# One decoder block: silu pairs in the middle, a second gate product asked for earlier, y in freed h tiles, v pieces on GpSimd's queue

## The chip, the core and the metric

The kernel runs on one core of one Trainium2 chip. A core has a matrix engine (TensorE, here PE, with its weight load PEld), a vector engine (DVE), a scalar engine (ACT), GpSimd (POOL) and SyncE (SP), which here only issues transfers. All of them work on tiles of 128 partitions in on-chip memory; 16 DMA engines move data between it and device memory. The engines run in parallel, each takes its instructions in order, and semaphores hold an instruction until what it needs is there. The metric is the device time of one execution, in microseconds.

## What is computed

A residual block over 1024 positions and 1024 channels, in float32:

```python
h = rmsnorm(x) * (1 + scale) + shift              # scale, shift, gate from c
q, k, v, g_attn, xr, g_rnn, m_attn, m_rnn = split(h @ w_in)
y_attn = window_attention(rope(q), rope(k), v, sinks) * silu(g_attn)
xr = causal_conv4(xr)
r, i = sigmoid(xr @ wa + ba), sigmoid(xr @ wx + bx)   # 4 blocks of 256 channels
a = exp(-8 * r * softplus(-lam))
state[t] = a[t] * state[t-1] + sqrt(1 - a[t]**2) * i[t] * xr[t]
y_rnn = state * silu(g_rnn)
merged = sigmoid(m_attn) * (y_attn @ w_ap) + sigmoid(m_rnn) * (y_rnn @ w_rp)
out = rmsnorm(x + gate * (merged @ w_out))
```

The attention has 16 heads of 64 in four groups (one k and v head for each), a window of 128 positions and a learned sink per head.

## The kernel before

Every float32 factor is split into a high part, rounded to the matrix engine's float32r format, and a low rest; a product is three matmuls (high x high, low x high, high x low). The split is one ACT cast (`cast`, line 101) and one DVE subtraction (`rest`, line 107).

**Pairs.** The wide projection is done in pairs of 128-column chunks (`Pair`, line 509). A pair is computed as a 2 x 2 block product with seven products instead of eight, so it takes seven slots of 12 matmuls (`product`, line 500, matmuls at line 505), at a planner's cost of 2.75 us a slot. In the seven slots it needs sums of weights (`tsum`, line 527), seven splits, and copies and differences of results (lines 554, 557, 565). Its weights are loaded six slots ahead (`r`, a ring of six tiles). Four sinks of a pair take a finished result of 128 x 512 each:

- a q pair applies the rotary embedding and stores q;
- a tanh pair (`MA`, `MR`, the merge gates; `tanh_sinks` with `silu` false) is one ACT tanh (line 608), whose result is stored (a sigmoid is made of it at the end);
- a silu pair (`GA`, `GR`) is a tanh on ACT and then one DVE instruction (line 613), whose result is stored;
- an `XR` pair collects two channel blocks for the recurrent branch, whose convolution is four steps (`base` on ACT, line 682, and three `tap`s on DVE, line 687).

There are 23 pairs. The list `pairs` (line 249) sets their order; the pair with index i starts at slot 7i. The last pair, MR[3], runs inside the attention stage.

**Recurrent branch.** For each of the four `XR` pairs there are two gate products (`extra`, line 764, matmuls at line 778), 24 matmuls into two PSUM tiles each; PSUM has two tiles for them, so that a second product overwrites what the sigmoids of the first have read. `after_gates` (line 785) is the chain behind a product: sigmoids (793, 796) and d1 (799), tanh (807) and d2 (803), exp and square (810, 813), d3 (816), square root (820), d4 (823), the scan (828), a product with the stored silu(g_rnn) (832), and the split of y, which is stored as `yh_d` and `yl_d` (835, 839). Chain 0 and chain 1 of a pair come one after the other. `start_gates` asks for product 1 after the step of chain 0 with index 3.

**Order.** A planner at build time writes the order of all engines. Fixed steps stand at a slot (`at_slot`); background steps wait in two lists (`waiting`) and are placed at a slot where the planned load of ACT and DVE (`Load`) leaves room (`background`, line 468). `slots(1)` in a list means that the next step comes at least one slot later; the last chains (hb = 3, "rush") have none between their steps. Where the lists are empty and slot 150 or so is reached, `open_attn` (line 968) starts attention.

**Attention stage.** There are 32 units of one group and 128 positions. In unit u the scores of u are made (line 1016), weights of u - 1 (1040), the values of u - 3 (1088) and the transposes of u - 2 (1054); POOL sets the sink column (`sink`, 1004) and the masks (1074). Between these PE takes one piece of other work a unit: the slots of the last pair, and then `rp_steps` (line 1150), the product of y with w_rp, in 32 pieces. SP loads ks and qs for every second unit, the two v factors (`load_v`, line 991, called from `values` at every second unit), the stored silu(g_attn), w_rp, and y: `load_y(0)` and `load_y(1)` go into tiles of h that are already free, chunks 2 to 7 into a ring `ypool` of 12 tiles. `store` (line 590) puts off the stores of this stage to the next `flush`, on SP. After attention come the w_ap products, the merge and the output product; the merged chunks are written to y's tiles (chunks 0 and 1) or to the ring.

Of the kernel before, what the change touches and what calls it, by code (L numbers as in the profile page):

```python
# [13 lines left out]
F32R = mybir.dt.float32r  # L14
# [8 lines left out]
P = 128  # L23
S = 1024
# [23 lines left out]
SL = [slice(0, HALF), slice(HALF, S)]  # L48
# [3 lines left out]
def tile_hybrid_block(ctx, tc, x, pk, rows, posr, posi, invf, c_row, w_ss, w_gate, w_main, w_v,  # L52
                      w_g, w_ap, w_rp, w_out, out):
    nc = tc.nc
# [83 lines left out]

    hba = ctx.enter_context(tc.tile_pool(name="hba", bufs=1))
    h_ctx = ExitStack()  # L140
    hb = h_ctx.enter_context(tc.tile_pool(name="hb", bufs=1))
    b12_ctx = ExitStack()
    b12 = b12_ctx.enter_context(tc.tile_pool(name="b12", bufs=1, side="right"))
    hh, hl = [], []
    for kc in range(KC):
        for lst, nm in ((hh, "hh"), (hl, "hl")):
            if kc < 4:
                a = hba.tile([P, HALF], F32R, name=f"{nm}a{kc}")
                b = b12.tile([P, HALF], F32R, name=f"{nm}b{kc}")
                lst.append([a[:], b[:]])  # L150
            else:
                a = hb.tile([P, S], F32R, name=f"{nm}{kc}")
                lst.append([a[:, SL[0]], a[:, SL[1]]])
    xx = b12_ctx.enter_context(tc.tile_pool(name="xx", bufs=1, side="right"))
    hx = h_ctx.enter_context(tc.tile_pool(name="hx", bufs=8))
    xT = [xx.tile([P, S], F32, name=f"xT{kc}") if kc % 4 == 3 else
# [444 lines left out]
    def tanh_sinks(dst, silu):  # L601
        def steps(j, th):
            def sink(s):
                t = {}

                def f1():
                    t["t"] = blk()
                    A.activation(t["t"], s(), AF.Tanh, scale=0.5)
                    if not silu:
                        store(dst[j][:, SL[th]], t["t"])  # L610

                def f2():
                    V.scalar_tensor_tensor(out=t["t"], in0=t["t"], scalar=1.0, in1=s(),
                                           op0=ALU.add, op1=ALU.mult)
                    store(dst[j][:, SL[th]], t["t"])

                return [("A", 0.62, 0, f1)] + ([("D", 0, 0.69, f2)] if silu else [])
            return sink
        return {"C11": steps(0, 0), "C12": (blk, steps(0, 1)), "C21": steps(1, 0),
                "C22": (blk, steps(1, 1))}  # L620
# [38 lines left out]
    def xr_sinks(hb):  # L659
# [15 lines left out]
        def conv(ic):  # L675
            def add(s):
                c, t = 2 * hb + ic, {}
                x_ = xr[ic]

                def base():  # L680
                    t["xc"] = W["rn"].tile([P, S], F32, tag="xc", name="xc", bufs=2)
                    A.activation(t["xc"][:], x_[:], AF.Identity,
                                 scale=pcol(PK_CW + 24, c), bias=pcol(PK_CB, c))

                def tap(k):
                    o = t["xc"][:, 3 - k:]
                    V.scalar_tensor_tensor(out=o, in0=x_[:, :S - 3 + k],
                                           scalar=pcol(PK_CW + 8 * k, c), in1=o,
                                           op0=ALU.mult, op1=ALU.add)

                def hi():
                    t["h"] = W["rn"].tile([P, S], F32R, tag="xa", name="xch", bufs=2)
                    A.copy(t["h"][:], t["xc"][:])

                def lo():
                    t["l"] = W["rn"].tile([P, S], F32R, tag="xcl", name="xcl", bufs=2)
                    V.tensor_tensor(out=t["l"][:], in0=t["xc"][:], in1=f32(t["h"][:]),
                                    op=ALU.subtract)
                    W["xc", hb, ic] = (t["h"], t["l"], t["xc"])

                taps = [("D", 0, 1.28, lambda k=k: tap(k)) for k in (2, 1, 0)]
                waiting[1].extend([[("A", 1.06, 0, base)], slots(1), *[[t_] for t_ in taps]])
                load0, split0 = gate_weights(hb, 0)
                if ic == 1:
                    waiting[1].append(load0)
                waiting[1].extend([slots(1), [("A", 1.06, 0, hi)], slots(1),
                                   [("D", 0, 1.22, lo)]])
                if ic == 1:
                    waiting[1].extend(split0 + [lambda: start_gates(hb)])
            return add  # L710
# [30 lines left out]
    def ask(hb, oc):  # L741
# [2 lines left out]
            gq.append((hb, oc))  # L744
        return ("g", (hb, oc)) in W

    def start_gates(hb):

        load1, split1 = gate_weights(hb, 1)
# [2 lines left out]
        one, two = [], [lambda: ask(hb, 1)]  # L752
        for todo, steps_ in ((one, c0), (two, c1)):
            for i, step in enumerate(steps_):
                todo.extend(step + ([slots(1)] if hb < 3 else []))
                if todo is one and i == 3:
                    todo.append(lambda: gq.append((hb, 1)) or True)
        if hb == 3:
            one.insert(0, lambda: W.setdefault("rush", True))
        waiting[0].extend(one + two)  # L760
# [2 lines left out]

    def extra():

        if not gq or Load.pe < W.get(("ready", *gq[0]), 1e9):
            return 0.0
        hb, oc = gq.pop(0)
        wh, wl = W["gw", hb, oc]
# [15 lines left out]
    def after_gates(hb, oc):  # L785
# [16 lines left out]
        def d2():  # L802
            V.tensor_tensor(out=t["it"][:], in0=t["it"][:], in1=W["xc", hb, oc][2][:],
                            op=ALU.mult)

        def a3():
            A.activation(tl("th"), t["rz"][:], AF.Tanh)
# [183 lines left out]
    def load_v(m):  # L991
        g, n0 = m // 4, (m % 4) * 2
        vs = at.tile([P, 2, P], F32R, tag="vs", name="vs", bufs=2)
        dv = at.tile([P, 2, P], F32R, tag="dv", name="dv", bufs=2)
        dma(dv[:], dv_d[g][:, n0:n0 + 2, :])
        lo = 0 if n0 else 1
        dma(vs[:, lo:, :], vs_d[g][:, n0 - 1 + lo:n0 + 1, :])
        U["v", m] = vs, dv

    def sink(u):  # L1000
# [134 lines left out]
    def load_y(c):  # L1135
        if c < 2:
# [3 lines left out]
                dma(ls[i], yl_d[c][:, SL[i]])  # L1140
            yh[c], yl[c] = hs, ls
            return
        h_ = W["yp"].tile([P, S], F32R, tag="Y", name="yh")
        l_ = W["yp"].tile([P, S], F32R, tag="Y", name="yl")
        dma(h_[:], yh_d[c])
        dma(l_[:], yl_d[c])
        yh[c] = [h_[:, SL[0]], h_[:, SL[1]]]
        yl[c] = [l_[:, SL[0]], l_[:, SL[1]]]

    def rp_steps():  # L1150
# [1 line left out]
        pb_ctx.close()  # L1152
        psr = pool(ctx, "psr", space=PSUM, side="right")
        rp_acc.extend(psr.tile([P, S], F32, name=f"rp{i}") for i in range(2))
        W["yp"] = pool(ctx, "ypool", bufs=12)
        W["tout"] = pool(ctx, "tout", bufs=1)
        W["hpool"] = pool(ctx, "hpool", bufs=7)

# [14 lines left out]

        seq = [(c, k) for k in range(4) for c in range(2)]
        seq += [(c, k) for c in range(2, KC) for k in range(4)]
        load_y(2)
        load_y(3)
        for i, (c, k) in enumerate(seq):
            part(c, k)
# [35 lines left out]
    def a_prep(m):  # L1215
# [13 lines left out]
        def f3():  # L1229
# [4 lines left out]
            else:  # L1234
# [11 lines left out]
    GR = [Pair(C_GR + 2 * g, tanh_sinks(sgr_d[2 * g:2 * g + 2], True)) for g in range(NG)]  # L1246
    XR = [Pair(C_XR + 2 * h, xr_sinks(h)) for h in range(4)]
    Q = [None] + [Pair(2 + 2 * g, rope_q(g), 0.125) for g in range(1, NG)]
    pairs = [Q[1], MA[0], Q[2], MA[1], Q[3],
             XR[0], GR[0], GR[1], XR[1], MA[2], GR[2], MR[0], XR[2], MR[1], MR[2], MA[3],  # L1250
             XR[3], GR[3]] + GA + MR[3:]
    N_ATT = 1
    def v_product(ps, th):
        for kc, i in [(kc, i) for j in range(2) for kc in range(KC) for i in (j, j + 2)]:
# [67 lines left out]
    while W["slot"] < 7 * (len(pairs) - N_ATT) + 1:  # L1322
# [1 line left out]
        flush()  # L1324

    s_last = 7 * len(pairs) - 7
    at_slot(s_last + 2, ("N", 0, 0, lambda: load_r(0)), ("N", 0, 0, lambda: load_y(0)),
            ("N", 0, 0, lambda: load_r(1)), ("N", 0, 0, lambda: load_y(1)),
            ("N", 0, 0, lambda: prep_r(0, 0)), ("N", 0, 0, lambda: prep_r(1, 0)))

    def fill():
        for _ in steps:
# [116 lines left out]
    for c in range(KC):  # L1449
# [17 lines left out]
        V.scalar_tensor_tensor(out=s_[:], in0=s_[:], scalar=1.0, in1=ps[:], op0=ALU.add,  # L1467
                               op1=ALU.mult)
        V.tensor_tensor(out=t[:], in0=t[:], in1=s_[:], op=ALU.add)
        if c < 2:  # L1470
            mh[c], ml[c] = yh[c], yl[c]
        else:
            mh[c], ml[c] = [
# [161 lines left out]
```

## Time and profile before

| | us |
|---|---|
| median of 3 runs | 946.4 (944.32 to 946.92) |
| profiled execution | 944.47 |
| its span, first to last instruction | 942.5 |
| PE busy | 908.1 (96%) |
| DVE busy | 688.8 (73%) |
| ACT busy | 528.8 (56%) |
| POOL busy | 89.7 (10%) |

The span lies 1.97 us under the time of the same execution. The profile names an instruction by engine, source line, operation and "out<-in". In the views of stages there is the busy time of each engine in a stretch of the span; in the views of waits, how long an engine stood still and which instruction released it; in the timeline, start, duration and in brackets the idle time ahead with its releaser. A transfer issued at SP has the engine name SPq. The stages lie as follows: start to about 101 us, pairs and recurrent branch to 570, attention from 570 to 760 (the last pair to 603, the w_rp products from 605), then the w_ap products and the merge to 845, and the output product.

### The profile page before, as it was taken

The numbers are of one execution on the slowest core, as the hardware profiler recorded it, in microseconds if no ns is written. First come the engines' busy times: TensorE is split into PE (matmuls) and PEld (weight loads), VectorE is DVE, ScalarE is ACT, GpSimd is POOL, SyncE is SP. The second block draws the span as 40 slices with busy tenths as digits, with TensorE's granted clock in tenths as the row PEclk, the third lists the DMA queues.
The fourth block names the chain that finished last, engine by engine and source line by source line (L and its number), as shares of the span: only waits on it lengthen the run. The fifth ranks groups of instructions, "written<-read, shape, count | busy, mean of one in ns | idle before, by whom it ended". The sixth has DMA issues, their size and how long they took to land.

```text
span 942.5 us, 12419 instructions
## 1 busy us (share of the span) xinstructions
PE 908.1 (96%) x4261; PEld 750.6 (80%) x4261; DVE 688.8 (73%) x1068; ACT 528.8 (56%) x1036; POOL 89.7 (10%) x129
## 2 busy tenths in 40 slices
PE   5899999999999999999999999989999999999997
PEld 3689777788888788888888778867888888887886
DVE  7977798876668955984688677888999737656522
ACT  7434654455556755866585775877888632212311
POOL 1056000000000000000000000233333300000000
PEclk9999999999999999999999999999999999999999
DMA  8923565753332433352334237897666286436321
GB/s 312 370 68 152 184 223 202 268 189 125 112 112 96 139 136 100 133 212 80 122 112 168 100 134 261 278 342 251 215 198 187 67 304 219 168 118 235 128 79 67
DMA packets 84275, 164.19 MB, mean 174 GB/s; under 512 B 12771, under 2 KB 33251, under 8 KB 84214
## 3 DMA queue, kind: packets, MB, share of 16 engines
q1 hardware_dynamic: 83350, 161.09, 49.8%
q0 software_dynamic: 720, 2.07, 0.6%
q8 instruction: 33, 0.54, 0.2%
q14 instruction: 28, 0.23, 0.1%
q10 hardware_dynamic: 144, 0.26, 0.1%
HBM read 114.00 MB, written 49.78 MB: 174 GB/s over the span
## 4 chain that ended last, share of the span: by engine, by line
PE 75%; ACT 4%; DMA 4%; DVE 4%; issue 2%; SPq 0%; POOL 0%; DVEq 0%; ACTq 0%
PE bk L505 39%; PE rp L168 12%; PE rp L1500 5%; PE pgate L778 5%; PE pmain L1500 4%; PE pmain L168 4%; PE s_ps L1016 3%; PE pv L1088 3%; PE pt L1054 1%; DMA dv<-dv_d 1%; DMA ks<-k_d 1%; DMA r<-w_rp 1%; ACT wh L101 1%; DMA r<-w_main 1%; DVE nl L390 1%
## 5 line engine op out<-in xcount | busy, mean ns | idle before, releaser
L505 PE MATMUL bk<-nh,wl 128*128 128x512 f32 x368 | 143.7, 391 | 2.0 <-DVE wl L107 1.9
L505 PE MATMUL bk<-nh,wh 128*128 128x512 f32 x368 | 143.4, 390 | 0.0
L505 PE MATMUL bk<-nl,wh 128*128 128x512 f32 x368 | 143.2, 389 | 0.0
L107 DVE TENSOR_TENSOR wl<-r,wh 128x512 fp32r<-128x512 f32 x108 | 79.1, 736 | 16.5 <-ACT wh L101 16.5
L101 ACT CAST wh<-r 128x512 fp32r<-128x512 f32 x108 | 66.5, 618 | 33.5 <-DMA r<-w_ap 11.3
L505 PEld LDWEIGHTS bk<-nh,wl 128*128 128x128 f32 x368 | 69.1, 188 | 17.7 <-DVE wl L107 3.1
L505 PEld LDWEIGHTS bk<-nh,wh 128*128 128x128 f32 x368 | 69.1, 188 | 15.2 <-ACT wh L103 0.9
L505 PEld LDWEIGHTS bk<-nl,wh 128*128 128x128 f32 x368 | 69.1, 188 | 14.3
L505 PE MATMUL bk<-hh,wl 128*128 128x512 f32 x184 | 71.7, 390 | 0.4 <-DVE wl L107 0.4
L505 PE MATMUL bk<-hl,wh 128*128 128x512 f32 x184 | 71.6, 389 | 0.0
L505 PE MATMUL bk<-hh,wh 128*128 128x512 f32 x184 | 71.6, 389 | 0.0
L107 DVE TENSOR_TENSOR wl<-ws,wh 128x512 fp32r<-128x512 f32 x80 | 54.1, 683 | 4.0 <-ACT wh L101 4.0
L101 ACT CAST wh<-ws 128x512 fp32r<-128x512 f32 x80 | 48.2, 616 | 4.8 <-DVE ws L527 3.0
L1040 ACT ACTIVATE p<-p,small 128x129 f32<-128x129 f32 x128 | 50.1, 400 | 0.0
L59 POOL DMA_DIRECT2D yh_d<-yh x1 | 0.6, 583 | 482.3 <-ACT yh L835 482.3
L505 PE MATMUL bk<-hha,wl 128*128 128x512 f32 x92 | 36.4, 395 | 5.9 <-DVE wl L107 4.4
L505 PEld LDWEIGHTS bk<-hh,wl 128*128 128x128 f32 x184 | 34.5, 188 | 7.9 <-DVE wl L107 0.8
L505 PEld LDWEIGHTS bk<-hh,wh 128*128 128x128 f32 x184 | 34.5, 188 | 7.2
L505 PEld LDWEIGHTS bk<-hl,wh 128*128 128x128 f32 x184 | 34.5, 188 | 7.1
L1016 PE MATMUL s_ps<-ks,qs 128*128 128x256 f32 (+1 forms) x256 | 37.5, 289 | 0.0
L1517 ACT ACTIVATE o<-xo 128x1024 f32<-128x1024 f32 (+2 forms) x10 | 8.9, 889 | 48.4 <-DVE xo L1516 48.4
L505 PE MATMUL bk<-hla,wh 128*128 128x512 f32 x92 | 35.9, 390 | 0.0
(338 smaller groups left out, 2231.7 us busy)
## 6 DMA issues: line engine op xcount, KB each, us to landing
r<-w_main SPq DMA_DIRECT2D x100, 256.0 KB, 4.0
wada<-w_ss SPq DMA_DIRECT2D x16, 512.0 KB, 8.6
qs<-q_d SPq DMA_DIRECT2D x16, 512.0 KB, 5.4
ks<-k_d SPq DMA_DIRECT2D x24, 192.0 KB, 4.1
xt<-x SPq DMA_DIRECT2D x8, 512.0 KB, 7.2
q_d<-rhi SPq DMA_DIRECT2D x16, 256.0 KB, 3.5
q_d<-rlo SPq DMA_DIRECT2D x16, 256.0 KB, 3.3
wg<-w_gate SPq DMA_DIRECT2D x8, 512.0 KB, 5.0
```

Of the source, the lines that this page charges most:

```text
L101: A.copy(dst[0][:], src)
L107: V.tensor_tensor(out=dst[1][:], in0=src, in1=f32(dst[0][:]), op=ALU.subtract)
L168: mm = T.matmul(ps[hf], ww, xx[kc][hf], start=(kc == 0 and ww is w_h and xx is xh), stop=(kc == KC - 1 and xx is xl))
L390: V.tensor_tensor(out=nl[t][:], in0=xT[t][:], in1=f32(nh[t][:]), op=ALU.subtract)
L505: W["pe"] = T.matmul(ps, ww[:, c], b[kc][xx_], start=(first and kc == 0 and i == 0), stop=(kc == 3 and i == 2), skip_group_check=not first)
L778: W["pe"] = T.matmul(ps[:, SL[hf]], ww[:, c0:c0 + P], xx_[:, SL[hf]], start=(ic == 0 and i == 0), stop=(ic == 1 and i == 2))
L1016: W["pe"] = T.matmul(o, qs[:, j, qc], ks[:, b, k0 + (0 if n else P):k0 + 256], start=(b == 0), stop=(b == 1))
L1040: A.activation(px[:, j, :], px[:, j, :], AF.Exp, bias=sm[:, 0, j:j + 1], accum_out=sm[:, 1, j:j + 1])
L1054: W["pe"] = T.transpose(pt[:, j, :], px[:, j, 0:P], ident[:])
L1088: W["pe"] = T.matmul(pv[:], b, m[:].rearrange("p j q -> p (j q)"), start=(i == 0), stop=(i == len(prods) - 1))
L1500: T.matmul(ps[:, sl], lhs[k][th][:, ts_], w[:, sl], start=(k == 0 and w is h_ and lhs is mh), stop=(k == KC - 1 and lhs is ml))
L1517: A.activation(o[:, sl], xo[:, sl], AF.Square, accum_out=fs[:, i:i + 1])
```

## The change

- The order of the pairs: all eight silu pairs stand between XR[0] and XR[3] now, and the six pairs behind XR[3] are tanh pairs. The XR pairs keep their places.
- Product 1 of a recurrent block is asked for after the step of chain 0 with index 1 (its two sigmoids); a planned time "free" holds it until the sigmoids are done. The last chains get one more `slots(1)`, behind their first step.
- The base of a convolution waits until the chain two blocks before has read the tile it will overwrite.
- Tiles hh4 to hh7 and hl4 to hl7 stay allocated; y chunks 2 to 5 are loaded there, and merged chunks 2 to 5 are written there. `ypool` has 4 tiles instead of 12. The loads of y(0), y(1) and y(2) are placed earlier.
- The two v loads of every second unit are issued by POOL instead of SP.
- Tanh results of the attention stage (the last pair) are stored by ACT, at once, instead of by SP at the next flush.

```diff
--- before.py
+++ after.py
@@ -138,10 +138,10 @@
 
     hba = ctx.enter_context(tc.tile_pool(name="hba", bufs=1))
     h_ctx = ExitStack()
-    hb = h_ctx.enter_context(tc.tile_pool(name="hb", bufs=1))
+    hb = ctx.enter_context(tc.tile_pool(name="hb", bufs=1))
     b12_ctx = ExitStack()
     b12 = b12_ctx.enter_context(tc.tile_pool(name="b12", bufs=1, side="right"))
-    hh, hl = [], []
+    hh, hl, whole = [], [], {}
     for kc in range(KC):
         for lst, nm in ((hh, "hh"), (hl, "hl")):
             if kc < 4:
@@ -151,6 +151,7 @@
             else:
                 a = hb.tile([P, S], F32R, name=f"{nm}{kc}")
                 lst.append([a[:, SL[0]], a[:, SL[1]]])
+                whole[nm, kc] = a[:]
     xx = b12_ctx.enter_context(tc.tile_pool(name="xx", bufs=1, side="right"))
     hx = h_ctx.enter_context(tc.tile_pool(name="hx", bufs=8))
     xT = [xx.tile([P, S], F32, name=f"xT{kc}") if kc % 4 == 3 else
@@ -607,7 +608,7 @@
                     t["t"] = blk()
                     A.activation(t["t"], s(), AF.Tanh, scale=0.5)
                     if not silu:
-                        store(dst[j][:, SL[th]], t["t"])
+                        dma(dst[j][:, SL[th]], t["t"], A if "att" in W else nc.sync)
 
                 def f2():
                     V.scalar_tensor_tensor(out=t["t"], in0=t["t"], scalar=1.0, in1=s(),
@@ -699,7 +700,8 @@
                     W["xc", hb, ic] = (t["h"], t["l"], t["xc"])
 
                 taps = [("D", 0, 1.28, lambda k=k: tap(k)) for k in (2, 1, 0)]
-                waiting[1].extend([[("A", 1.06, 0, base)], slots(1), *[[t_] for t_ in taps]])
+                waiting[1].extend([lambda: c < 2 or ("used", c - 2) in W,
+                                   [("A", 1.06, 0, base)], slots(1), *[[t_] for t_ in taps]])
                 load0, split0 = gate_weights(hb, 0)
                 if ic == 1:
                     waiting[1].append(load0)
@@ -744,6 +746,12 @@
             gq.append((hb, oc))
         return ("g", (hb, oc)) in W
 
+    def second(hb):
+
+        gq.append((hb, 1))
+        W["free", hb, 1] = Load.act + 0.4
+        return True
+
     def start_gates(hb):
 
         load1, split1 = gate_weights(hb, 1)
@@ -752,9 +760,9 @@
         one, two = [], [lambda: ask(hb, 1)]
         for todo, steps_ in ((one, c0), (two, c1)):
             for i, step in enumerate(steps_):
-                todo.extend(step + ([slots(1)] if hb < 3 else []))
-                if todo is one and i == 3:
-                    todo.append(lambda: gq.append((hb, 1)) or True)
+                todo.extend(step + ([slots(1)] if hb < 3 or i == 0 else []))
+                if todo is one and i == 1:
+                    todo.append(lambda: second(hb))
         if hb == 3:
             one.insert(0, lambda: W.setdefault("rush", True))
         waiting[0].extend(one + two)
@@ -763,7 +771,8 @@
 
     def extra():
 
-        if not gq or Load.pe < W.get(("ready", *gq[0]), 1e9):
+        if not gq or Load.pe < max(W.get((n_, *gq[0]), d_) for n_, d_ in (
+                ("ready", 1e9), ("free", 0.0))):
             return 0.0
         hb, oc = gq.pop(0)
         wh, wl = W["gw", hb, oc]
@@ -802,6 +811,7 @@
         def d2():
             V.tensor_tensor(out=t["it"][:], in0=t["it"][:], in1=W["xc", hb, oc][2][:],
                             op=ALU.mult)
+            W["used", c] = True
 
         def a3():
             A.activation(tl("th"), t["rz"][:], AF.Tanh)
@@ -992,9 +1002,9 @@
         g, n0 = m // 4, (m % 4) * 2
         vs = at.tile([P, 2, P], F32R, tag="vs", name="vs", bufs=2)
         dv = at.tile([P, 2, P], F32R, tag="dv", name="dv", bufs=2)
-        dma(dv[:], dv_d[g][:, n0:n0 + 2, :])
+        dma(dv[:], dv_d[g][:, n0:n0 + 2, :], G)
         lo = 0 if n0 else 1
-        dma(vs[:, lo:, :], vs_d[g][:, n0 - 1 + lo:n0 + 1, :])
+        dma(vs[:, lo:, :], vs_d[g][:, n0 - 1 + lo:n0 + 1, :], G)
         U["v", m] = vs, dv
 
     def sink(u):
@@ -1140,10 +1150,12 @@
                 dma(ls[i], yl_d[c][:, SL[i]])
             yh[c], yl[c] = hs, ls
             return
-        h_ = W["yp"].tile([P, S], F32R, tag="Y", name="yh")
-        l_ = W["yp"].tile([P, S], F32R, tag="Y", name="yl")
-        dma(h_[:], yh_d[c])
-        dma(l_[:], yl_d[c])
+        if c < 6:
+            h_, l_ = whole["hh", c + 2], whole["hl", c + 2]
+        else:
+            h_, l_ = (W["yp"].tile([P, S], F32R, tag="Y", name=n_)[:] for n_ in ("yh", "yl"))
+        dma(h_, yh_d[c])
+        dma(l_, yl_d[c])
         yh[c] = [h_[:, SL[0]], h_[:, SL[1]]]
         yl[c] = [l_[:, SL[0]], l_[:, SL[1]]]
 
@@ -1152,7 +1164,7 @@
         pb_ctx.close()
         psr = pool(ctx, "psr", space=PSUM, side="right")
         rp_acc.extend(psr.tile([P, S], F32, name=f"rp{i}") for i in range(2))
-        W["yp"] = pool(ctx, "ypool", bufs=12)
+        W["yp"] = pool(ctx, "ypool", bufs=4)
         W["tout"] = pool(ctx, "tout", bufs=1)
         W["hpool"] = pool(ctx, "hpool", bufs=7)
 
@@ -1173,7 +1185,6 @@
 
         seq = [(c, k) for k in range(4) for c in range(2)]
         seq += [(c, k) for c in range(2, KC) for k in range(4)]
-        load_y(2)
         load_y(3)
         for i, (c, k) in enumerate(seq):
             part(c, k)
@@ -1246,9 +1257,8 @@
     GR = [Pair(C_GR + 2 * g, tanh_sinks(sgr_d[2 * g:2 * g + 2], True)) for g in range(NG)]
     XR = [Pair(C_XR + 2 * h, xr_sinks(h)) for h in range(4)]
     Q = [None] + [Pair(2 + 2 * g, rope_q(g), 0.125) for g in range(1, NG)]
-    pairs = [Q[1], MA[0], Q[2], MA[1], Q[3],
-             XR[0], GR[0], GR[1], XR[1], MA[2], GR[2], MR[0], XR[2], MR[1], MR[2], MA[3],
-             XR[3], GR[3]] + GA + MR[3:]
+    pairs = [Q[1], MA[0], Q[2], MA[1], Q[3], XR[0], GR[0], GA[0], XR[1], GR[1], GA[1], GR[2],
+             XR[2], GA[2], GA[3], GR[3], XR[3], MA[2], MA[3]] + MR
     N_ATT = 1
     def v_product(ps, th):
         for kc, i in [(kc, i) for j in range(2) for kc in range(KC) for i in (j, j + 2)]:
@@ -1324,9 +1334,10 @@
         flush()
 
     s_last = 7 * len(pairs) - 7
-    at_slot(s_last + 2, ("N", 0, 0, lambda: load_r(0)), ("N", 0, 0, lambda: load_y(0)),
-            ("N", 0, 0, lambda: load_r(1)), ("N", 0, 0, lambda: load_y(1)),
-            ("N", 0, 0, lambda: prep_r(0, 0)), ("N", 0, 0, lambda: prep_r(1, 0)))
+    at_slot(s_last + 2, [("N", 0, 0, lambda: load_r(0)), ("N", 0, 0, lambda: load_y(0))],
+            ("N", 0, 0, lambda: load_y(1)), ("N", 0, 0, lambda: load_r(1)), [],
+            [("N", 0, 0, lambda: prep_r(0, 0)), ("N", 0, 0, lambda: load_y(2))],
+            ("N", 0, 0, lambda: prep_r(1, 0)))
 
     def fill():
         for _ in steps:
@@ -1467,7 +1478,7 @@
         V.scalar_tensor_tensor(out=s_[:], in0=s_[:], scalar=1.0, in1=ps[:], op0=ALU.add,
                                op1=ALU.mult)
         V.tensor_tensor(out=t[:], in0=t[:], in1=s_[:], op=ALU.add)
-        if c < 2:
+        if c < 6:
             mh[c], ml[c] = yh[c], yl[c]
         else:
             mh[c], ml[c] = [
```

## The prediction

> **What bounds the kernel now.** I read the page first, then busy time by stage, then PE's waits, then the DMA issues of SP's queue around the worst stage.
>
> ```profile
> span 942.5 us, 12419 instructions
> ```
> ```profile
> 292.00:330.00 38.00, 37.55 (x166) 30.78 (x165) 35.25 (x43) 31.18 (x44) 0.00 (x0) 1.00 0.43 140
> 330.00:520.00 190.00, 190.00 (x840) 157.26 (x839) 136.54 (x176) 123.58 (x173) 0.00 (x0) 1.00 0.38 132
> 520.00:570.00 50.00, 46.70 (x201) 37.00 (x200) 37.02 (x45) 36.90 (x48) 0.47 (x1) 1.00 0.36 126
> 570.00:615.00 45.00, 44.98 (x244) 38.32 (x243) 36.51 (x66) 33.27 (x102) 9.44 (x20) 1.00 0.85 280
> 615.00:640.00 25.00, 20.59 (x107) 16.01 (x106) 20.24 (x36) 15.58 (x52) 6.52 (x10) 1.00 1.04 358
> ```
> The columns are length, then busy time of PE, PEld, DVE, ACT and POOL, the clock, the DMA share and GB/s. PE is the bound, at full clock, and the change adds or removes no matmul. So it can only win PE's idle time in the stages it touches: 0.45 in 292 to 330, none in 330 to 520, 3.3 in 520 to 570, 0.02 + 4.41 in 570 to 640, together 8.2 us. The start, and the products after attention, keep their order. The two large holes have these owners (520 to 570 first, then 600 to 760; total, times, longest):
>
> ```profile
> PE bk L505 <- DVE wl L107: 3.3, 4, 1.2
> ```
> ```profile
> PE pv L1088 <- DMA dv<-dv_d: 1.8, 1, 1.8
> PE pv L1088 <- DVE small L1035: 1.4, 1, 1.4
> PE rp L168 <- DMA yl<-yl_d: 0.6, 1, 0.6
> PE rp L168 <- DMA yh<-yh_d: 0.5, 1, 0.5
> ```
>
> **The hole in 615 to 640.** The DMA issues on SP, and the products that wait:
>
> ```profile
> 604.09 0.47 SPq L59 DMA_DIRECT2D vs<-vs_d  x1
> 608.89 1.56 SPq L59 DMA_DIRECT2D smr_d<-c  x2
> 610.50 0.42 SPq L59 DMA_DIRECT2D yh<-yh_d  x1
> ...
> 617.82 0.32 SPq L59 DMA_DIRECT2D dv<-dv_d  x1
> 619.63 0.32 SPq L59 DMA_DIRECT2D vs<-vs_d  x1
> ```
> ```profile
> 595.05 2.75 PE bk L505 x12
> ...
> 605.14 2.75 PE rp L168 x12
> ...
> 629.90 9.02 DMA dv<-dv_d
> ```
> Twelve y loads of 512 KB (chunks 2 to 7) start only at 610.50, behind the smr_d stores for whose tanh SP stood from 604.56 to 608.89. The 16 DMA engines are then full (share 1.04, 358 GB/s), and the v pieces queue behind y: the vs of 619.63 is the likely owner of the 1.4 us put down to a DVE instruction long done, and one dv took 9.02 us.
>
> The change moves four things here. First, y(0) is issued one piece of PE's filler earlier, with w_rp, and y(1) two pieces earlier. Secondly, y(2) goes into h tiles 4. Their last product is the second half of A12 and S4 of the last pair, ended before the x12 at 595.05, so y(2) can be issued near 598, a stage ahead of 610.50. Thirdly, the four smr_d stores leave SP for ACT, which frees 608.89 - 604.56 = 4.3 us of SP; y(3) can go out near 605, when the rp products start. Fourthly, the 32 v loads leave SP.
>
> Is there room? 570 to 615 has a share of 0.85 at 280 GB/s: 15% of 45 us at 280/0.85 = 329 GB/s is 2.2 MB, and y(2) is 1.05 MB. Of y(2) and y(3), three of four pieces were still under way at 615 (PE waits for yl, then yh; 1.6 MB); taken out of the full stretch at 358 GB/s that is 4.4 us, as much as the hole of 4.41. But the remaining stages of it get closer together when PE no longer waits, so I leave 0.8 us: gain 3.6, bounds 0 (the transfers only collide elsewhere) and 4.4.
>
> **The v loads on POOL.** POOL's prices and slack:
>
> ```profile
> L1074 POOL TENSOR_SCALAR_AFFINE_SELECT plm<-plc 128x512 fp32r<-128x512 f32 x28 | 27.4, 977 | 14.3 <-DVE plc L1065 14.3
> L1074 POOL TENSOR_SCALAR_AFFINE_SELECT phm<-phc 128x512 fp32r<-128x512 f32 x28 | 17.8, 635 | 32.2 <-ACT phc L1059 32.2
> L1004 POOL COPY p<-sink 128x4 f32<-128x4 f32 x32 | 7.1, 225 | 72.7 <-PE pt L1054 57.2 <-issue 15.4
> L59 POOL DMA_DIRECT2D yh_d<-yh x1 | 0.6, 583 | 482.3 <-ACT yh L835 482.3
> ```
> ```profile
> yl_d<-yl POOLq DMA_DIRECT2D x1, 512.0 KB, 7.2
> ```
> ```profile
> 640.19 0.95 PE s_ps L1016 x8
> ...
> 645.23 0.95 PE s_ps L1016 x8
> ```
> A unit takes 645.23 - 640.19 = 5.04 us; every second one issues a dv and a vs. They stand in POOL's order after the masks of the unit and ahead of the sink copy of the next but one, which waits 72.7 us in all: 32 x 0.58 = 18.7 us fits there, and without this cover would delay masks by at most 1.2 us each second unit. What they overwrite was last read one unit earlier. They are needed two units later, in 10.1 us; issue 1.2 plus the 7.2 of a transfer four times as large is 8.4. So they are in time, at no cost.
>
> The row speaks of a danger: plm, which runs beside DVE's copies of the same stage, takes 977 ns where phm of the same shape takes 635, so POOL is slowed beside DVE by 977/635 = 1.54. [...]
>
> The four stores on ACT cost it at the row of SP's issues (0.32 each, 1.3 us together) in 70 us with 21 idle: nothing.
>
> New waits, and what stands behind them: y(2) on SP waits for S4 of the last pair (behind it the next ks, qs and gate pieces; it is over before the issue). A v load on POOL waits for the products of the unit before (behind it the sink copy and the masks, for which PE waits; over too). A store on ACT waits for its own tanh (behind it casts of weights).
>
> **The hole in 520 to 570.** The drain of the last gates, with the wait in brackets:
>
> ```profile
> 547.80 1.28 DVE L799 SCALAR_TENSOR_TENSOR rz<-rz,pk_t,rbig 128x1024 f32<-128x1024 f32 x1 [3.85 <-ACT rz L793]
> ```
> ```profile
> 550.94 0.50 PE L505 MATMUL bk<-hha,wl 128*128 128x512 f32 x1 [1.08 <-DVE wl L107]
> ```
> ```profile
> 558.38 1.23 DVE L816 SCALAR_TENSOR_TENSOR th<-rz,th 128x1024 f32<-128x1024 f32 x1 [2.75 <-ACT rz L813]
> ```
> ```profile
> 516.07 5.46 PE pgate L778 x24
> ...
> 536.04 5.44 PE pgate L778 x24
> ```
> DVE is 74% busy, not full; it stands in order behind ACT, and the weight split (wl) behind it comes late. Three edits bear on it. The pairs after XR[3] become plain tanh pairs, which have no L613 on DVE: four of 0.68 us a pair, 2.6 pairs, 7.1 us less. The step added after the first sigmoid puts L799 a slot (2.75 us) later, so that most of its 3.85 us of waiting, and the 1.08 that PE lost behind it, go. The second product is asked for after two steps instead of four, so it follows its first closer than 536.04 - 516.07 = 20 us; its result then waits for ACT, not ACT for it. What stays is the wait for L813 (2.75), since the rush has no further slot between L813 and L816. Of the four waits of PE I keep the one before 561 (1.2): gain 2.1, bounds 0 and 3.3.
>
> **The middle pays.** The same L613 go to the stretch from XR[1] to XR[3]: of its six other pairs one was a silu pair, now all six are. By slots of 2.75 us their sinks fall between about 300 and 455 us (an estimate).
>
> ```profile
> L613 DVE SCALAR_TENSOR_TENSOR c<-c x16: 680/684/687, 241.8 to 580.8; 128x512 f32<-128x512 f32 x16
> ```
> ```profile
> 400.00:420.00 20.00, 20.00 (x90) 16.56 (x89) 19.35 (x23) 13.98 (x20) 0.00 (x0) 1.00 0.56 199
> 420.00:440.00 20.00, 20.00 (x90) 16.54 (x89) 8.55 (x13) 10.88 (x16) 0.00 (x0) 1.00 0.28 99
> ```
> That is 20 x 0.684 = 13.7 us more of DVE, in a load that is uneven: 97% before a first gate product, 43% behind it. The planner holds background steps back when its count of DVE is full, so the surplus runs into the thin part (11.4 us idle in 420 to 440 alone) before PE sees it: 20 us at 97% cost PE nothing, 38 us at 93% (292 to 330) cost 0.45. With a fuller second half of the chains I take two more holes of 0.45, 0.9 us; bounds 0 and 6.6 (two holes like the drain's 3.3). Past 455 us DVE has five silu pairs less, so the last chain should not end later. The guard on the conv base only puts off a step of ACT that would have stood waiting for its buffer.
>
> Freed h tiles for y and merged: same bytes, same splits, no work; ypool shrinks by what stays held.
>
> **Sum.** 3.6 + 2.1 - 0.9 = 4.8 us. The profiled execution took 944.47 (span 942.5 and 1.97 around it): 939.7. The median of the runs is 946.4, 1.9 above that execution; a gain of 4.8 on it gives **941.6**.
>
> **Rivals.**
> - All is won: both holes close and the middle is free: 946.4 - 8.2 = 938.2. For it: DVE's thin parts have room. Against: L816 still waits for L813. 0.12.
> - The transfers move their collision: y(0) to y(2) now meet kq and v loads of 575 to 605, and 570 to 615 has a share of 0.85 already; of the 4.4 nothing is gained: 946.4 - 2.1 + 0.9 = 945.2. An engine order that turns out as before (second product no earlier) ends near the same. 0.16.
> - The middle becomes a drain: two holes of 3.3 beside both gains: 946.4 - 5.7 + 6.6 = 947.3. For it: DVE is at 97% in 400 to 420 before any silu pair is added. Against: no such hole in 330 to 520 now. 0.11.
> - Slower: v comes late from POOL. Place: products L1088 of every second unit. Two issues stretched 1.54 times take 1.8 us; with the 9.02 us that a dv took here that is 10.8, 0.7 over the 10.1 allowed; it decides where landing is above 8.3 us. 15 pieces x 0.7 = 10.5: 946.4 - 2.1 + 0.9 + 10.5 = 955.7 with no gain in the hole. Against: off SP's ring a v piece needn't stand behind y. [...] 0.09.
>
> **How the numbers follow.** The forecast has 0.52, with its own range 939 to 944 from its bounds. No change within 0.3% (2.8 us, about what a measurement of this kernel can tell) is 943.6 to 949.2. Faster: 0.12 and 0.48 of the forecast, 0.60. Same: 0.04 of it, 0.16, and 0.08 of the third rival: 0.28. Slower: 0.09 and 0.03 of the third: 0.12. For 8 in 10 the range goes from the first rival to the third with its bound: 938 to 948.
>
> **What would show it.** PE idle below 1.5 us in the attention's first 65 us, y loads of chunk 2 issued a stage before the rp products, dv and vs on POOL landing in under 8 us, no SP wait for the last tanh; PE idle below 2 us between the last gates and attention; at most 1 us of waits for wl in the middle. It is wrong if PE waits for dv or vs in steady units, or for wl before the last gates, by more than 2 us.

## The result and the profile after

The changed kernel takes 942.1 us in the median against 944.14 of the kernel before, measured side by side: a ratio of 0.9977, 95% interval 0.9967 to 0.9987, or 2.0 us less. The time itself is close to the 941.6 forecast, but it was reached with less than half of the forecast gain of 4.8: the earlier median of 946.4 came from three runs, and twenty runs beside the changed kernel gave 944.14. By the prediction's own measure a change of 2.0 us lies within the 2.8 that it called no change, to which it gave 0.28. The parts of the sum have to be judged one by one.

The profiled execution of the changed kernel took 944.67, the longest of its twenty and 2.6 above their median, so a loss seen in it need not be in the others. Its span, and then the busy time in the stages that the prediction used (the columns are the same):

```profile
span 942.9 us, 12429 instructions
```
```profile
292.00:330.00 38.00, 38.00 (x169) 31.45 (x169) 36.07 (x47) 30.71 (x43) 0.00 (x0) 1.00 0.41 143
330.00:520.00 190.00, 189.63 (x837) 156.47 (x836) 140.39 (x180) 128.14 (x177) 0.00 (x0) 1.00 0.39 132
520.00:570.00 50.00, 46.59 (x195) 36.94 (x194) 34.90 (x41) 36.75 (x48) 1.81 (x4) 0.97 0.42 139
570.00:615.00 45.00, 45.00 (x240) 38.34 (x238) 31.47 (x57) 30.74 (x91) 11.06 (x21) 1.00 0.91 301
615.00:640.00 25.00, 24.42 (x135) 20.44 (x134) 24.19 (x45) 20.97 (x70) 12.76 (x21) 1.00 1.02 342
```

PE's idle time in 615 to 640 fell from 4.41 to 0.58 us. The middle lost its hole (0.45 to 0). The drain in 520 to 570 did not improve: 3.3 us idle before, 3.41 now, and its mean granted clock is now 0.97 instead of 1.00; ahead of it a new wait of 0.37 stands at 505.77.

**The attention's hole.** PE's waits in 600 to 640, two of the y issues on SP, and the v issues on POOL (busy time, mean ns of one, idle time before):

```profile
PE pv L1098 <- POOL plm L1084: 0.4, 1, 0.4
PE s_ps L1026 <- DVE p L1040: 0.2, 1, 0.2
```
```profile
594.94 0.56 SPq L59 DMA_DIRECT2D hh<-yh_d  x1
...
604.60 0.62 SPq L59 DMA_DIRECT2D hh<-yh_d  x1
```
```profile
L59 POOL DMA_DIRECT2D dv<-dv_d x16 | 8.9, 559 | 0.6 <-DMA hla<-yl_d 0.5
L59 POOL DMA_DIRECT2D vs<-vs_d x16 | 8.6, 537 | 0.0
```

No wait for dv, yl or yh is left. y(2) is issued at 594.94 and y(3) at 604.60 instead of at 610.50 and 611.47. The v pieces on POOL land in at most 7.5 us; from SP a dv took up to 9.02.

**The drain.** DVE and PE after, with the wait in brackets, and then the same part of DVE's order before:

```profile
546.94 1.29 DVE L808 SCALAR_TENSOR_TENSOR rz<-rz,pk_t,rbig 128x1024 f32<-128x1024 f32 x1 [1.01 <-ACT rz L802]
...
551.67 0.69 DVE L107 TENSOR_TENSOR wl<-ws,wh 128x512 fp32r<-128x512 f32 x1
552.27 0.69 DVE L528 TENSOR_TENSOR ws<-r 128x512 f32<-128x512 f32 x1
555.84 1.23 DVE L826 SCALAR_TENSOR_TENSOR th<-rz,th 128x1024 f32<-128x1024 f32 x1 [2.88 <-ACT rz L823]
556.99 0.69 DVE L107 TENSOR_TENSOR wl<-r,wh 128x512 fp32r<-128x512 f32 x1
559.72 1.23 DVE L833 SCALAR_TENSOR_TENSOR it<-th,it 128x1024 f32<-128x1024 f32 x1 [2.05 <-ACT th L830]
```
```profile
557.73 0.50 PE L506 MATMUL bk<-nh,wl 128*128 128x512 f32 x1 [2.30 <-DVE wl L107]
569.12 0.50 PE L506 MATMUL bk<-hh,wl 128*128 128x512 f32 x1 [1.11 <-DVE wl L107]
```
```profile
553.14 0.68 DVE L107 TENSOR_TENSOR wl<-ws,wh 128x512 fp32r<-128x512 f32 x1
...
554.34 0.69 DVE L107 TENSOR_TENSOR wl<-r,wh 128x512 fp32r<-128x512 f32 x1
...
561.75 1.23 DVE L823 SCALAR_TENSOR_TENSOR it<-th,it 128x1024 f32<-128x1024 f32 x1 [0.33 <-ACT th L820]
```

The wait of 3.85 behind the first sigmoid shrank to 1.01, as forecast. But before, two weight splits (wl) stood in DVE's order ahead of L816; now only one stands ahead of its successor L826, and the next comes behind it at 556.99. PE waits 2.30 us for that one. L833, which had waited 0.33, now waits 2.05: before, a silu step, a weight split and a weight sum (559.53 to 561.42) stood between L816 and it; now one split does, and DVE arrives earlier.

**Behind the attention.** In order of time, the DVE step of the merge, the first output product of PE and SP's load of its next weights, with PE's wait in 840 to 865; two fences after, then two before:

```profile
839.32 1.23 DVE L1476 SCALAR_TENSOR_TENSOR tt<-smr,tt 128x1024 f32<-128x1024 f32 x1 [5.05 <-DMA smr<-smr_d]
844.62 1.07 PE L1511 MATMUL rp<-wo,hha 128*128 128x512 f32 x4
844.94 0.33 SPq L59 DMA_DIRECT2D wo<-w_out  x1
```
```profile
PE rp L1511 <- ACT wo L1446: 2.4, 1, 2.4
```
```profile
846.66 0.33 SPq L59 DMA_DIRECT2D wo<-w_out  x1
847.43 1.07 PE L1500 MATMUL rp<-wo,hha 128*128 128x512 f32 x4
```
```profile
PE rp L1500 <- ACT wo L1435: 0.8, 1, 0.8
```

PE arrives 2.81 us earlier (844.62 against 847.43), but the load of wo only 1.72 us earlier. It stands on SP behind the merge, whose DVE step waits 5.05 us for smr; that tile has one buffer, so its load cannot start earlier. From the start of this product to the end of the span it takes 98.3 us after and 95.1 before: in this execution 3.2 us of what had been won up to there are given back, 1.6 as a longer wait and the rest as a slower clock. Not every execution does so: in the seven runs below that keep the one tile for smr, this wait is at most 0.5 us, and from the product to the end it takes 94.5 to 96.1. Four windows show the clock (last but two of the columns) behind two gaps, 2.30 us in the drain and 2.41 us here:

```profile
556.00:560.00 4.00, 2.27 (x8) 1.86 (x9) 1.95 (x3) 3.97 (x6) 0.00 (x0) 0.87 0.57 175
560.00:564.00 4.00, 4.00 (x14) 3.09 (x13) 4.00 (x4) 3.07 (x5) 0.00 (x0) 0.70 0.47 150
852.00:854.00 2.00, 2.00 (x7) 1.58 (x7) 1.97 (x3) 0.00 (x0) 0.00 (x0) 0.63 0.38 113
854.00:856.00 2.00, 2.00 (x7) 1.52 (x6) 1.31 (x2) 1.10 (x2) 0.00 (x0) 0.51 0.97 369
```

The clock is 0.50 for 3.41 us in each place, 558.99 to 562.40 and 852.54 to 855.95, and PE is busy throughout; half of that, 1.7 us each, is an estimate of the work that PE loses. PE is counted as busy there, so the idle time alone hides it. In the drain, though, the slow clock cost no time. Its 80 us before, after, and in the run with the v pieces on SP, whose drain is the same:

```profile
500.00:580.00 80.00, 76.70 (x337) 61.94 (x337) 57.74 (x76) 52.18 (x73) 1.77 (x4) 1.00 0.46 161
500.00:580.00 80.00, 76.22 (x325) 60.96 (x323) 52.90 (x64) 53.17 (x72) 2.56 (x5) 0.98 0.53 179
500.00:580.00 80.00, 74.74 (x322) 59.40 (x321) 52.81 (x64) 52.93 (x72) 1.54 (x3) 1.00 0.51 172
```

At full clock PE idles 5.3 us there, near the 5.5 that 3.8 of idle time and 1.7 of slow clock make together. From the first gate product of the last recurrent block to the first score product it takes 66.1 us with the slow clock and 66.5 without: at full speed PE only waits longer afterwards. So this drain loses some 2 us more than the 3.3 of before, whatever the clock.

### The profile page after: what moved, and what is told of

Same layout as the page of the kernel before. It is cut to its first block, busy times and chain, and to the rows that moved or that the text cites. A ratio compares the mean times of both kernels' runs of the same rounds, so it can differ in the third digit from the quotient of the medians.

```text
span 942.9 us, 12429 instructions
## 1 busy us (share of the span) xinstructions
PE 910.3 (97%) x4261; PEld 753.2 (80%) x4261; DVE 688.4 (73%) x1068; ACT 532.3 (56%) x1038; POOL 109.1 (12%) x161
```

## The experiments

Each ratio is to the kernel before, with its 95% interval. The kernels differ from the changed kernel by the diff shown.

**The three edits ahead of the attention.** First the v pieces alone go back to SP.

```diff
-        dma(dv[:], dv_d[g][:, n0:n0 + 2, :], G)
+        dma(dv[:], dv_d[g][:, n0:n0 + 2, :])
...
-        dma(vs[:, lo:, :], vs_d[g][:, n0 - 1 + lo:n0 + 1, :], G)
+        dma(vs[:, lo:, :], vs_d[g][:, n0 - 1 + lo:n0 + 1, :])
```

> The changed kernel, with the v loads back on SP. The prediction's step: v queues behind y on SP, so PE waits for dv or vs in the attention's first units come back, 1.5 to 3 us in 600 to 640, and the time rises by as much. Rival: the earlier y loads and the stores on ACT already empty the queue: waits stay under 0.7 us, time within 0.5 us of the changed kernel.

Measured: 943.99, ratio 1.0001 [0.9988, 1.0013], 1.9 over the changed kernel; PE idles 1.1 us in 600 to 640, and there is no wait for dv or vs. The time is the theory's; the waits for v that it rests on are not there.

Then only the y loads are as late as before:

```diff
+        load_y(2)
         load_y(3)
...
-    at_slot(s_last + 2, [("N", 0, 0, lambda: load_r(0)), ("N", 0, 0, lambda: load_y(0))],
-            ("N", 0, 0, lambda: load_y(1)), ("N", 0, 0, lambda: load_r(1)), [],
-            [("N", 0, 0, lambda: prep_r(0, 0)), ("N", 0, 0, lambda: load_y(2))],
-            ("N", 0, 0, lambda: prep_r(1, 0)))
+    at_slot(s_last + 2, ("N", 0, 0, lambda: load_r(0)), ("N", 0, 0, lambda: load_y(0)),
+            ("N", 0, 0, lambda: load_r(1)), ("N", 0, 0, lambda: load_y(1)),
+            ("N", 0, 0, lambda: prep_r(0, 0)), ("N", 0, 0, lambda: prep_r(1, 0)))
```

> The changed kernel with only the y loads as late as before (y(2) at the start of the output products, y(0) and y(1) a piece of filler later); v stays on POOL and the last tanh stores on ACT. Theory (the early y loads carry most of the gain of the hole): PE idles 2 to 4 us more in 600 to 640 than its 0.6, the waits stand at the output products for yl or yh and not for dv; 944 to 946. Rival (v on its own queue alone is enough, since dv and vs then stand behind nothing): below 1 us more, 942 to 943.

Measured: 944.27, ratio 1.0001 [0.9990, 1.0012]; the idle time in 580 to 640 grows by 1.4 us. The time is as the theory has it; the waits are not, since they are spread over several small ones (0.9 for phc, 0.4 for plm, 0.3 for u, 0.2 for plc), and none of them is for y.

Then both, and the last tanh stores on SP again:

```diff
-                        dma(dst[j][:, SL[th]], t["t"], A if "att" in W else nc.sync)
+                        store(dst[j][:, SL[th]], t["t"])
```

> The changed kernel with the three edits ahead of the attention undone together: the v pieces and the last tanh stores are issued on SP again, and y(2) is loaded at the start of the output products. Theory (the 3.9 us that 600 to 640 won come from these three edits, whichever carries most): PE idles at least 3.5 us in 600 to 640 again, with waits for dv, yl or yh, and the median is 945 to 947. Rival (the hole closed because the earlier stages sit differently, and the edits only go with it): idle below 1.5 us, 942 to 943.

Measured: 946.05, ratio 1.0021 [1.0007, 1.0034], 3.95 over the changed kernel. PE's waits in 600 to 640, and the window:

```profile
PE pv L1098 <- DMA vs<-vs_d: 3.5, 2, 2.3
PE rp L169 <- DMA hh<-yh_d: 0.5, 1, 0.5
PE rp L169 <- DMA hl<-yl_d: 0.4, 1, 0.4
```
```profile
600.00:640.00 40.00, 35.60 (x186) 29.26 (x185) 31.60 (x58) 27.22 (x88) 12.89 (x20) 0.96 0.92 298
```

The 4.4 us of idle time are back, with waits for v and y as in the kernel before, so it was these edits that filled the hole. Undone singly, v and y each cost about 2 us of time (943.99 and 944.27 against 942.1), but little of it shows as a wait; where it is lost isn't shown. The stores were not undone alone.

**The order of pairs and the second product.** The old order with the new second product:

```diff
-    pairs = [Q[1], MA[0], Q[2], MA[1], Q[3], XR[0], GR[0], GA[0], XR[1], GR[1], GA[1], GR[2],
-             XR[2], GA[2], GA[3], GR[3], XR[3], MA[2], MA[3]] + MR
+    pairs = [Q[1], MA[0], Q[2], MA[1], Q[3],
+             XR[0], GR[0], GR[1], XR[1], MA[2], GR[2], MR[0], XR[2], MR[1], MR[2], MA[3],
+             XR[3], GR[3]] + GA + MR[3:]
```

> The changed kernel with the old order of pairs (silu pairs behind XR[3] again). Prediction's theory (five silu pairs less in the drain free DVE there): the idle time of 500 to 580 grows by 2 to 4 us over the 3.8 idle and 1.6 of half clock of the changed kernel, and 292 to 330 idles 0.45 again; 944 to 946. Rival (the drain hangs on the chain of ACT and DVE through the last gates, which no silu sink lies on): the drain keeps 4.5 to 5.5 us, 942 to 943; if it falls to 3.3, the new order made the drain worse, 940 to 941.

Measured: 943.97, ratio 1.0002 [0.9989, 1.0015]. PE's waits in 500 to 580:

```profile
PE bk L506 <- DVE wl L107: 6.0, 3, 2.9
```

The idle time grew by 2.2 us, as the prediction's theory has it, and 292 to 330 idles 0.3 again; the time lies at the lower edge of what it gives. With the slot and the earlier second product in place, the silu pairs in the drain do cost; without those two edits they don't, as the kernel before shows with 3.3.

The new order with the old second product, and without the slot behind the first sigmoid:

```diff
-                todo.extend(step + ([slots(1)] if hb < 3 or i == 0 else []))
-                if todo is one and i == 1:
-                    todo.append(lambda: second(hb))
+                todo.extend(step + ([slots(1)] if hb < 3 else []))
+                if todo is one and i == 3:
+                    todo.append(lambda: gq.append((hb, 1)) or True)
```

> The changed kernel with the second gate product asked for after four steps as before, and without the slot behind the first sigmoid in the last half block. Theory (these two edits put the last chain later, and DVE and ACT now end together later: the first s_ps came at 580.08 against 578.00): idle time and half clock of 500 to 580 fall from 5.4 to about 3.3 us, 940 to 941, and DVE's first add waits some 3.8 us for the sigmoid again. Rival (the silu order sets it, not these): still 4.5 to 5.5 us, 942 to 943. Prediction's theory (the two edits help): 6 us or more, 943 to 944.

Measured: 950.42, ratio 1.0068 [1.0051, 1.0084], a clear miss of all three expectations. The loss begins in the middle, where the changed kernel had none:

```profile
330.00:500.00 170.00, 166.00 (x718) 135.10 (x717) 122.41 (x159) 106.56 (x149) 0.00 (x0) 0.99 0.35 120
```

That is 4.0 us of idle time, with a slow clock behind one of the gaps (0.98 in 400 to 500). The two gate products of a recurrent block start 21.8 us apart again (349.21 and 370.97), against 13.6 in the changed kernel (347.12 and 360.72), and the last block's first one starts at 523.62 instead of 513.83. So the middle does not bear the silu pairs as such; it bears them because the second product comes 8 us earlier.

Then neither edit: order, second product, slot and the guard on the conv base all as before, and only the edits ahead of the attention left.

> The changed kernel with the order of pairs, the second gate product, the slot and the conv guard all as before, so that only the edits ahead of the attention are left. Theory (order and second product work only as a pair: undone alone they cost 1.9 and 8.3 us, together the middle and the drain were as good before them): drain idle 3.3 us and one middle hole of 0.45 as in the kernel before, 600 to 640 nearly full; the median lies 3 to 4.5 below the kernel before, 939 to 941, at or below the changed kernel's 942.1. Rival (the two edits are each worth what undoing them alone cost): 945 or more.

Measured: 940.65, ratio 0.9964 [0.9952, 0.9976]. The theory held: 3.3 us under the kernel before and 1.45 under the changed kernel (the two intervals just overlap). Its drain and its attention:

```profile
520.00:570.00 50.00, 46.65 (x201) 36.97 (x200) 36.82 (x45) 36.85 (x49) 0.26 (x1) 1.00 0.35 125
...
615.00:640.00 25.00, 24.51 (x135) 20.67 (x136) 24.19 (x44) 21.01 (x70) 13.58 (x21) 1.00 1.03 334
```

The drain idles 3.35 as before, at full clock. Order alone or second product alone costs more than both together, and both together gain nothing.

**The drain.** A free slot behind the exp and square of the last recurrent block too:

```diff
-                todo.extend(step + ([slots(1)] if hb < 3 or i == 0 else []))
+                todo.extend(step + ([slots(1)] if hb < 3 or i in (0, 3) else []))
```

> The changed kernel, with one more slot between the exp and square of the last chains (steps with index 3) and the DVE step behind them. Theory: the 2.30 us for which PE waits at 555 to 558 us in the changed kernel come from DVE standing 2.88 us in order behind ACT's table load, exp and square, and the idle time is followed by 3.4 us at half clock (1.7 us more). Then that wait goes below 0.8 us, the clock in 556 to 564 stays at 1.00, and the time falls by 3 to 4 us against the changed kernel (942.1): 938 to 939. Rival: ACT is the bound of the drain, and the wait only comes a slot later: less than 1 us.

Measured: 942.66, ratio 0.9988 [0.9975, 1.0000]: no gain. Nearly all waits of PE in the drain became one:

```profile
563.91 0.50 PE L506 MATMUL bk<-hh,wl 128*128 128x512 f32 x1 [3.82 <-DVE wl L107]
```

Then, with the second tile of the next experiment, the costs with which the order is worked out, set to what the trace shows:

```diff
-                [[("A", 2.35, 0, a3)], [("D", 0, 1.22, d2)]],
-                [[("A", 1.06, 0, a4), ("A", 1.06, 0, a5)]], [[("D", 0, 1.22, d3)]],
+                [[("A", 1.06, 0, a3)], [("D", 0, 1.22, d2)]],
+                [[("A", 2.35, 0, a4), ("A", 1.06, 0, a5)]], [[("D", 0, 1.22, d3)]],
```

> The changed kernel with the second tile for the merge, and with two costs of the order's bookkeeping set to what the trace shows: the tanh of the gates 1.06 in place of 2.35 (no table load stands before it), the exp 2.35 in place of 1.06 (a table load of 1.28 stands before it). No instruction is added or removed. Theory (in the drain ACT is booked 1.28 us short, so that weight casts come behind the exp and square and PE waits for wl): idle time and half clock of 500 to 580 fall from 5.2 to 3 us or less, 938 to 939 against 940.2 with the second tile alone. Rival (the chain of ACT and DVE through the last gates sets the drain, whatever is booked): 4.5 to 5.5 us again, 940 to 941.

Measured: 941.35, ratio 0.9972 [0.9959, 0.9985], not below the second tile alone; PE's waits in 500 to 580 are 4.2 us, and the clock of 540 to 560 is 0.91. And the same with two more slots:

```diff
-                todo.extend(step + ([slots(1)] if hb < 3 or i == 0 else []))
+                todo.extend(step + ([slots(1)] if hb < 3 or i in (0, 3, 5) else []))
```

> The same bookkeeping and second tile, and a free slot behind the square and behind the square root of the last half block too, so that no DVE step of the last chains is issued in the slot of the ACT step that it waits for. Theory (DVE stands in order behind ACT, and wl behind it): DVE's waits for rz and th fall below 1 us each, PE idles under 2 us in 500 to 580, and if the attention opens no later, 937 to 938.5. Rival (as with the slot behind the square alone, the stalls only move to where the last scan and the last casts stand): 4 to 5 us in 500 to 600, 940 to 941.5.

Measured: 945.99, ratio 1.0022 [1.0010, 1.0034]. The waits for rz and th, 1.8 and 1.9 us, did not go below 1, and a new one came, first in DVE's row and then in PE's:

```profile
572.30 1.22 DVE L842 TENSOR_TENSOR rz<-rz,gg 128x1024 f32<-128x1024 f32 x1 [3.99 <-DMA gg<-sgr_d]
```
```profile
576.57 0.80 PE L506 MATMUL bk<-nh,wl 128*128 128x512 f32 x1 [5.19 <-DVE wl L107]
```

DVE reaches the product with gg before the load has landed, and wl stands behind it; the time is worse than the rival's too. In all three the theory fell: the stall comes back at another DVE step that waits and has a wl behind it. What in the chain would have to change isn't settled.

**The wait for wo.** A second tile for smr:

```diff
-        r_ = tpool.tile([P, S], F32, tag="sr", name="smr", bufs=1)
+        r_ = (ypool.tile([P, S], F32, tag="Y", name="smr") if c % 2 else
+              tpool.tile([P, S], F32, tag="sr", name="smr", bufs=1))
```

> The changed kernel, with a second tile for the smr loads of the merge (odd chunks use the y ring). Theory: after attention the merge is a chain of its own (one smr tile, two tt tiles, on SP), which gained only 1.7 us where PE gained 2.8; so the w_out chunk that PE needs at 849 comes too late, 2.41 us instead of 0.77 before, again with half clock behind it. Then the wait for wo falls below 0.8 us, the clock in 852 to 856 stays at 1.00, and the time falls by 3 us against the changed kernel: about 939. Rival: the two tt tiles set the chain, and smr has no part in it: wait still above 2 us, same time.

Measured: 940.23, ratio 0.9957 [0.9942, 0.9971], 1.9 under the changed kernel, of the 3 that its theory gave (the two intervals just overlap). No wait for wo is left, and the clock stays full:

```profile
840.00:860.00 20.00, 20.00 (x89) 16.55 (x89) 11.06 (x11) 3.25 (x4) 0.00 (x0) 1.00 0.64 237
```

With the slot of the drain as well:

> The changed kernel with both edits: the slot in the last chains and the second smr tile. If both waits are separate, the gains add: 6 us under the changed kernel, near 936, ratio to the kernel before 0.991. If PE's gain in the drain makes the merge chain late again, only half of it: 938 to 939.

Measured: 941.66, ratio 0.9969 [0.9957, 0.9981]; above both expectations: no wait for wo, but a drain wait of 3.50. And the second tile on the kernel that keeps only the edits ahead of the attention:

> The same with a second tile for the recurrent factors of the merge (odd chunks in a tile of the y ring). Theory: the wait for wo behind the recurrent product goes, 1 to 2 us less than without it: 937.5 to 939.5, the best so far. Rival (without the merge standing at its first product there is no wait for wo to win): the same time as without it within 0.5 us.

Measured: 938.92, ratio 0.9945 [0.9927, 0.9963]: 5.0 us under the kernel before, the best of all. The wait that it removes is only 0.3 in the profiled execution of the kernel without it, where the rival expected nothing to win; the 1.7 us between the medians have overlapping intervals, so its size here is uncertain. The third comparison, with the slot of the drain, gives 1.0 (942.66 and 941.66). All three point the same way, and from the first product with wo to the end it takes 94.0 us in each of the five runs with the second tile.

## Why the prediction was right, and where it was not

**The attention's hole (gain 3.6, bounds 0 to 4.4): right.** Idle time fell by 3.8 us, and the kernel with only these edits is 3.3 us faster; in its profile the stretch from the first score product to the first product with wo is 3.3 us shorter too (269.6 and 266.3). That v moves at no cost held too: POOL's issues took 559 and 537 ns, near the 0.58 used. On ACT there are eight stores, not four, of 0.33 us each. That the v move only makes room, and the y loads carry the gain, did not hold: undone alone, each costs about 2 us of time. The sixteen issues of dv lie between 546 and 562 ns and those of vs between 534 and 544, also in 615 to 640, where DVE is busy for 24.19 of 25 us: the 1.54 that the prediction takes from plm does not show in them.

**The middle (loss 0.9, bounds 0 to 6.6): right in its bounds, 1.4 off in size.** It cost nothing, and even the old 0.45 went. The reason given, that DVE's thin parts take the surplus, is half of it: without the earlier second product the same order idles PE for 4.0 us in 330 to 500, with a slow clock besides (0.98 in 400 to 500): the third rival's case, with 4.0 idle in place of 6.6. The prediction put the second product only in the drain; its worth lies in the middle.

**The drain (gain 2.1, bounds 0 to 3.3): wrong.** It lost some 2 us, outside the bounds: 5.3 us in 500 to 580 as idle time at full clock, 5.5 with a slow clock in it, against 3.3. The failing step is "most of its 3.85 us of waiting, and the 1.08 that PE lost behind it, go", with "the one before 561 (1.2)" as all that stays. The wait at the first sigmoid went, to 1.01. But in the new order of DVE one of two wl stands behind the next waiting step, so that the 1.2 became 2.30, and with fewer steps ahead of it L833 waits 2.05 where there had been 0.33. That the wl behind a waiting step makes PE wait is read from the timeline; whether the slot or the earlier second product put it there is open, since the runs undo the two only together. "7.1 us less" of DVE was no gain, because DVE was not short of time there (busy for 37.02 of 50 us before) but stood in order. The second product of the last recurrent block hardly came closer either: 19.3 us (513.83 and 533.09) against 20.

**The products after the attention (no term): the step that was missing.** "The start, and the products after attention, keep their order" is true, but nothing was said about whether what feeds them would come earlier too. In the profiled execution the merge's chain of loads did not by as much, and it took 1.6 us as a wait and 1.7 as a slow clock; the others show 0.5 at most of that wait. A second tile gave 1.9, 1.7 and 1.0 us. An earlier PE alone doesn't explain the 2.41: with the old order of pairs PE is as quick from the first score product to this one (264.8 us against 264.7), and the load of wo is issued 2.10 us ahead of the product, not 0.32 behind it. What held the merge back beyond its wait for smr (5.05 us, 4.71 before) is open.

**The sum.** Attention 3.3 by the kernel that has only its edits; order, second product and slot -1.45 instead of +1.2 (the two intervals just overlap; in the profiles -2.0 in the drain and +0.45 in the middle); together 1.85, measured 2.0. Both parts are taken from one kernel, so that they add up proves nothing more. That the forecast of 941.6 came so near 942.1 is luck: the gain was 2.8 us too large, and the median of before that it was taken from 2.3 us too high.

## What to carry over

Before crediting an edit that takes work off an engine, look whether the engine is full or stands in order behind another; in the second case ask what stands behind the next waiting instruction, and a slot put in front of one wait can move the queue behind it to the next. When an early stage gets shorter, follow each input of the next stages (here the loads of the merge, through a tile with one buffer) and ask whether it comes earlier by the same time. Edits that lean on each other, like the order and the second product, must be undone singly and together before either is given a price.

## What was not expected of the hardware

After some gaps of about 2 us the clock granted to PE fell to 0.50, for 3.41 us each time in the changed kernel; after others it stayed. Of the longest gaps in the drain, the attention and behind it in these profiles, a clock of 1.00 was kept after 1.82, 2.11, 2.31, 2.35 and 2.69 us, and a lower one followed 1.79, 2.22, 2.25, 2.26, 2.30, 2.41, 2.93, 3.50, 3.82 and 5.19 us (each with a mean of 0.83 to 0.91 in the 20 us around it). In the middle of the run with the old second product matmuls slowed down even behind 1.46 us, with another 0.45 some 2 us ahead: seven of them from 473.26 on take 0.63 us, against 0.39 from 476.55. What it cost depended on what PE waited for next: an estimated 1.7 us in the output product, where PE is the bound, and nothing to be seen in the drain, where DVE is late anyway (66.1 us with the slow clock and 66.5 without). The length of a gap alone doesn't settle which of the two follows, since 2.30 and 2.31 us ended differently; what does isn't shown.
